# Keys transposed in fp32 two groups at once and split afterwards, the third column block copied out of PSUM, the second keys one group later

## The chip, the core and the metric

The kernel runs on one core of a Trainium2 chip. The metric is the device time of one execution in microseconds, as the median of several runs. The core has five engines that work side by side: TensorE (PE in the profile; its weight loads are PEld), VectorE (DVE), ScalarE (ACT), GpSimd (POOL) and SyncE (SP), which here only issues DMAs. Matrix products land in PSUM, eight banks of 128 partitions by 512 fp32 columns; everything else lives in SBUF.

## The reference

The model is an encoder of two layers over 1024 positions of width 1024: attention and an MLP, then a gated MLP and an MLP. The change lies in the first layer's attention, of which this is what matters:

```python
def gqa_attention(h, w_qkv, q_g, k_g, w_o, cos, sin):
    qkv = h @ w_qkv                                   # 1024 x (1024 + 256 + 256)
    q, k, v = jnp.split(qkv, [Q_WIDTH, Q_WIDTH + KV_WIDTH], axis=-1)
    q = apply_rope(rmsnorm(q.reshape(B, T, N_HEADS, HEAD_DIM), q_g), cos, sin)
    k = apply_rope(rmsnorm(k.reshape(B, T, N_KV_HEADS, HEAD_DIM), k_g), cos, sin)
    ...
    s = jnp.einsum('bqkgd,bskd->bkgqs', q_blk, k).astype(jnp.float32) * scale
    p = jax.nn.softmax(s, axis=-1).astype(v.dtype)
    return jnp.einsum('bkgqs,bskd->bqkgd', p, v)
```

There are 16 query heads and 4 key heads of 64 columns; each key head serves a group of four query heads.

## The kernel before

Products of fp32 precision are made of float32r products: each operand is split into a high part (the value cast to float32r) and a low part (the value minus the high part), and three products are summed: high by high, high by low, low by high. So each split costs a cast, on ScalarE, and a subtraction, mostly on VectorE.

The projection is cut in two halves of 512 positions (`hs` and `hs1` hold the split activations) and three column blocks of 512: block 0 is keys and values (256 + 256 columns), blocks 1 and 2 are the queries. `qkv_mm(cb, kp, ps, hp)` (L568) issues the 24 products of block `cb` for one pair `kp` of the eight depth slices, into four PSUM banks of 128 positions each; four calls make a block. `banks(False)` takes four banks of the pool that `bank_x` serves, `banks(True)` both buffers of the score pool `ps_s` (two of two banks each, also served one at a time by `bank_s`). So at most one block of each kind is under way, and the next block of that kind waits until everything that reads the banks of the last has been read.

The blocks run in this order, first half: 0 and 1 together, then 2, into `ps` of the score pool; second half: 0 (`pk`), 1 (`pq`, score pool), 2 (`ps`). What is done with a block:

- values (`values`, L605): split by ScalarE (L610) and VectorE (L611), straight out of PSUM.
- keys: copied out (`k_copies`, L588), roped by VectorE (`k_rows`, L657), scaled by GpSimd (`k_scale`, L660; the scale comes from squares on ScalarE, L622, and sums on VectorE, L623). The tile holds two blocks of 128 positions by 256 columns.
- then `k_split` (L665) writes each key head twice side by side, once as high parts (ScalarE, L671) and once as low parts (VectorE, L672): eight tiles of 128 x 512 for each half. `kstacks` (L676) transposes these: for each of four heads and for high and low, four float32r transposes of 128 x 128 (L681) into a bank, and a copy (L683) into a tile of `kst`. Each `kst` tile is then a head's keys, 64 rows, stacked twice over 512 positions.
- queries: block 1 is copied out of PSUM (`q_copies`, L597); block 2 of the first half (`ps` at L826 to L829) is not: its squares (L622) and its ropes (L633 and L635 on VectorE, with L636 adding on GpSimd) read PSUM. `qk_scale` (L649) scales on GpSimd.

The score stage (`s_stage`, L943) multiplies query tiles, which hold high and low parts stacked in 128 rows, by a head's two `kst` tiles of each half. The first queries get there through `q_stage` (L918), which splits them on GpSimd (L925, L926), and `q_trans` (L930), two groups of four transposes (L934) and a copy. `q_stage(0, 0)` and `q_trans` are called after `qkv_mm(2, 1, ps, hs1)`, and the first scores after `qkv_mm(2, 2, ...)`.

The order on each engine comes from a planner: it simulates the program and issues, among the instructions that are ready by its own costs, the one that comes first in the program. Slots of the tile pools (58 of tag `t`, 16 of tag `x`) are handed out as they come free. An instruction may be pinned behind the one traced before it on its engine: `hold` does so up to L822, and `pin` in the attention's stages (L934, L948, L965 and others). The projection's products of the second half, `kstacks`, the ropes and the splits are not pinned. The attention proper is an order written out by hand, over 64 units of one query head and 256 queries each.

Of the kernel before, what the change touches and what calls it, by code (L numbers as in the profile page):

```python
# [12 lines left out]
F32R = mybir.dt.float32r  # L13
AF = mybir.ActivationFunctionType
ALU = mybir.AluOpType
# [3 lines left out]
P = 128  # L19
# [5 lines left out]
NKV = 4  # L25
HD = 64
# [10 lines left out]
def encoder_kernel(ctx: ExitStack, tc: tile.TileContext, t: dict, out: bass.AP):  # L37
# [22 lines left out]
    def slot(dt=F32, shape=(P, 512)):  # L60
        return mem.tile(list(shape), dt, tag="t", name=nm("t"), bufs=SLOTS["t"])

    def xslot(dt=F32):
        return mem.tile([P, 512], dt, tag="x", name=nm("x"), bufs=SLOTS["x"])
# [21 lines left out]
    def f32(ap):  # L86
        return ap.bitcast(F32)
# [451 lines left out]
    kst = {}  # L539
# [3 lines left out]
    if True:  # L543
# [53 lines left out]
        def q_copies(ps):  # L597
            raws = []
            for j in range(4):
                raw = slot()  # L600
                S.copy(raw, ps[j])
                raws.append(raw)
            return raws
# [11 lines left out]
        def heads(ap, nt=1):  # L615
            return ap.rearrange("p (t h d) -> p t h d", t=nt, d=HD)
# [27 lines left out]
        def q_sums(src):  # L644
            return qk_rstd(qk_sums(src))
# [5 lines left out]
        def q_rope(hf, cb, src, r, js, add=None):  # L651
            for j in js:
                d = qk_rope(src[j], 0, hf * 4 + j, 1, V, add)
                qk_scale(d, r, j)
                qn[(hf * 4 + j, cb - 1)] = d

        def k_rows(hf, src):  # L657
            return [qk_rope(src[j], 1, hf * 4 + 2 * j, 2) for j in range(2)]
# [3 lines left out]
            for j in range(2):  # L662
                qk_scale(kd[j], r, j)

        def k_split(kd):  # L665
            kk = []
            for j in range(4):
                kh, kl = slot(F32R), slot(F32R)
                src = heads(kd[j // 2], 2)[:, j % 2].unsqueeze(2).broadcast_to([P, NKV, 2, HD])
                hv = kh.rearrange("p (g s d) -> p g s d", g=NKV, s=2)  # L670
                S.copy(hv, src)  # L671
                V.tensor_tensor(kl.rearrange("p (g s d) -> p g s d", g=NKV, s=2), src, f32(hv), ALU.subtract)  # L672
                kk.append((kh, kl))
            return kk

        def kstacks(hf, kk, bank):  # L676
            for g in range(NKV):
                for s in range(2):
                    pt = bank("kt", dt=F32R)
                    for j in range(4):  # L680
                        T.transpose(pt[:, j * P : (j + 1) * P], kk[j][s][:, g * P : (g + 1) * P], identr)  # L681
                    d_ = xslot(F32R)
                    S.copy(d_, f32(pt))  # L683
                    kst[(g, hf, s)] = d_

        row = wide("c")
        nc.sync.dma_start(row[0:1, :], t["cond"])
# [135 lines left out]

        pk = banks(False)
        qkv_mm(0, 0, pk, hs1)
        rr2 = q_sums(ps)  # L826
        q_rope(0, 2, ps, rr2, (0, 1), G)
        qkv_mm(0, 1, pk, hs1)
        q_rope(0, 2, ps, rr2, (2, 3), G)  # L829
        qkv_mm(0, 2, pk, hs1)  # L830
        qkv_w(2, 0, V, True)
        kk = k_split(kd)
        qkv_mm(0, 3, pk, hs1)
        rk = k_copies(pk)
        values(1, pk)
        pq = banks(True)
        qkv_mm(1, 0, pq, hs1)
        kd = k_rows(1, rk)
        qkv_w(2, 1, V, True)
        qkv_mm(1, 1, pq, hs1)  # L840
        kstacks(0, kk, bank_x)
        k_scale(kd, rk)
        kk = k_split(kd)
        qkv_mm(1, 2, pq, hs1)
        qkv_w(2, 2, V, True)
        q_rope(0, 1, r1, rr, (0, 1))
        qkv_mm(1, 3, pq, hs1)
        qkv_w(2, 3, V, True)
        r3 = q_copies(pq)
        kstacks(1, kk, bank_x)  # L850
        ps = banks(False)
        qkv_mm(2, 0, ps, hs1)
        q_rope(0, 1, r1, rr, (2, 3))
        rr = q_sums(r3)
        r1 = r3
# [60 lines left out]
    with ExitStack() as es:  # L916
# [127 lines left out]
        for j in range(4):  # L1044
            deferred[10 + j] = lambda j=j: late_rope1(j)
            deferred[2 + 2 * j] = lambda j=j: late_sums(j)
            deferred[3 + 2 * j] = lambda j=j: late_rope(j)
        del hs, hs1, xs, xs1, rb, rb1, ps, pk, pq, rk, kk, kd, sq0, sq1, wq, r3
        for i in range(nu + 2):
            u0 = units[i] if i < nu else None  # L1050
            u1 = units[i - 1] if 0 < i <= nu else None
# [799 lines left out]
```

## Time and profile before

| | |
|---|---|
| median of 3 runs | 2628.07 us (2626.15, 2628.07, 2628.24) |
| span of the profiled execution | 2625.8 us |
| the profiled execution's own time | not listed apart from the three runs; the span lies 0.35 us under the fastest of them |
| TensorE busy | 2601.6 us (99%) |
| VectorE, ScalarE, GpSimd busy | 2183.1, 1451.1, 723.2 us (83, 55, 28%) |
| mean granted TensorE clock | 0.999 |
| projection's second half and the start of the attention | about 90 to 170 us of the span |

How to read the lines shown below. A group's line has the source line, engine, operation, output and input names, shapes and count, then the busy time, the mean ns of one, and the idle time of the engine just before it with what ended it. A line of the timeline has its start in us, its length, engine, source line, operation and how many instructions are merged; a bracket gives the idle time before it and what ended that. Matmuls are pipelined and their shown lengths overlap, so the distance from start to start is what counts. A row of a stretch has its bounds and length, then the busy us of PE, PEld, DVE, ACT and POOL with the number of instructions, the granted clock (1.00 is full), the DMA share and GB/s. Where a line such as L575 is reached from many calls, the tile names tell which: `qkv<-s,t` and `qkv<-w,t` have their weights in the kept buffers (block 0, and block 2 in the second half), `qkv<-t,t` is block 1, and block 2 in the first half.

### The profile page before, as it was taken

Reading aid. Unit: us, or ns where it says so; the run is one execution under the profiler, and the core shown is the slowest. Engines: PE = TensorE matmul, PEld = TensorE weight load, DVE = VectorE, ACT = ScalarE, POOL = GpSimd, SP = SyncE. Lnnn points to the kernel's source line nnn. Section 1 sums busy time; section 2 is a strip of 40 time slices with the busy share of each in tenths; the row PEclk is TensorE's granted clock in tenths of the full one; section 3 lists DMA queues with packets and bytes.
Section 4 is the critical chain, followed back from the end, with each engine's and each line's share of the span. In section 5 each row is a group of like instructions: output and inputs, shape, how many; then the busy total and the mean of one; then the engine's idle time right before and its main releaser. Section 6 shows DMA issues by size and latency. Waiting matters only on the chain. (4 is left out here: it accounts for less than half of the span.)

```text
span 2625.8 us, 37307 instructions
## 1 busy us (share of the span) xinstructions
PE 2601.6 (99%) x12860; PEld 2172.2 (83%) x12860; DVE 2183.1 (83%) x3276; ACT 1451.1 (55%) x2612; POOL 723.2 (28%) x531
## 2 busy tenths in 40 slices
PE   9999999999999999999999999999999999999999
PEld 7789999888788888888888888888888788888887
DVE  7868999887989989877897687788979977789974
ACT  4569999854654455446543354445456645465442
POOL 0238776533000004430122054451520000005400
PEclk9999999999999999999999999999999999999999
DMA  8010222234486788545243355568641554487461
GB/s 306 27 33 9 74 88 75 97 112 145 168 288 245 270 310 306 192 133 172 82 136 121 120 174 175 178 204 305 237 141 50 177 179 156 153 310 268 149 211 58
DMA packets 208752, 435.39 MB, mean 166 GB/s; under 512 B 23025, under 2 KB 35441, under 8 KB 208562
## 3 DMA queue, kind: packets, MB, share of 16 engines
q1 hardware_dynamic: 181682, 395.24, 44.7%
q10 hardware_dynamic: 26880, 37.76, 4.0%
q8 instruction: 102, 1.67, 0.3%
q14 instruction: 88, 0.72, 0.1%
HBM read 310.23 MB, written 122.68 MB: 165 GB/s over the span
## 5 line engine op out<-in xcount | busy, mean ns | idle before, releaser
L1212 PE MATMUL out<-t,s 128*128 128x512 f32 x1232 | 479.9, 390 | 0.9 <-ACT t L328 0.8
L1213 PE MATMUL out<-t,s 128*128 128x512 f32 x1232 | 479.3, 389 | 0.7 <-DVE t L329 0.7
L1214 PE MATMUL out<-t,s 128*128 128x512 f32 x1232 | 478.9, 389 | 0.0
L469 PE MATMUL w<-t,s 128*128 128x512 f32 x1168 | 459.8, 395 | 0.9 <-ACT t L328 0.5
L470 PE MATMUL w<-t,s 128*128 128x512 f32 x1168 | 455.2, 390 | 1.8 <-DVE t L329 1.8
L471 PE MATMUL w<-t,s 128*128 128x512 f32 x1168 | 454.7, 389 | 0.0
L329 DVE TENSOR_TENSOR t<-t,t 128x512 fp32r<-128x512 f32 x408 | 324.7, 806 | 36.2 <-ACT t L328 29.0
L328 ACT CAST t<-t 128x512 fp32r<-128x512 f32 x408 | 245.3, 617 | 122.2 <-DMA t<-hf 71.7
L1213 PEld LDWEIGHTS out<-t,s 128*128 128x128 f32 x1232 | 231.2, 188 | 50.2 <-DVE t L329 1.8
L1212 PEld LDWEIGHTS out<-t,s 128*128 128x128 f32 x1232 | 231.2, 188 | 50.2 <-ACT t L328 1.7
L1214 PEld LDWEIGHTS out<-t,s 128*128 128x128 f32 x1232 | 231.2, 188 | 48.1
L454 ACT CAST s<-w 128x512 fp32r<-128x512 f32 x292 | 173.4, 616 | 161.4 <-PE w L471 104.3
L470 PEld LDWEIGHTS w<-t,s 128*128 128x128 f32 x1168 | 219.3, 188 | 49.7 <-DVE t L329 5.2
L469 PEld LDWEIGHTS w<-t,s 128*128 128x128 f32 x1168 | 219.3, 188 | 49.4 <-issue 2.9
L471 PEld LDWEIGHTS w<-t,s 128*128 128x128 f32 x1168 | 219.2, 188 | 45.6
L455 DVE TENSOR_TENSOR s<-w,s 128x512 fp32r<-128x512 f32 x292 | 221.8, 766 | 41.1 <-ACT s L454 40.6
L1194 ACT CAST s<-t 128x512 fp32r<-128x512 f32 x240 | 148.2, 620 | 187.0 <-PE out L1214 136.3
L1180 POOL TENSOR_TENSOR w<-w,t 128x512 f32<-128x512 f32 x20 | 34.2, 1721 | 767.7 <-DMA t<-hf 691.5
L1195 DVE TENSOR_TENSOR s<-t,s 128x512 fp32r<-128x512 f32 x240 | 195.1, 814 | 56.1 <-ACT s L1194 55.4
L951 DVE TENSOR_REDUCE mx<-s 128x1 f32<-128x1024 f32 x128 | 156.2, 1220 | 30.5 <-PE s L948 29.2
L974 DVE TENSOR_TENSOR t<-t,t 128x512 fp32r<-128x512 f32 x256 | 164.1, 681 | 17.1 <-ACT t L968 16.4
L984 PE MATMUL o<-t,t 128*128 128x256 f32 x1024 | 162.6, 291 | 0.0
(251 smaller groups left out, 5089.1 us busy)
## 6 DMA issues: line engine op xcount, KB each, us to landing
t<-hf SPq DMA_DIRECT2D x320, 256.0 KB, 4.0
hf<-c SPq DMA_DIRECT2D x156, 256.0 KB, 3.4
w<-in_wi_dram SPq DMA_DIRECT2D x64, 512.0 KB, 4.5
hf<-c ACTq DMA_DIRECT2D x96, 256.0 KB, 2.7
w<-in_ada_dram SPq DMA_DIRECT2D x36, 512.0 KB, 3.9
x<-in_ada_dram SPq DMA_DIRECT2D x64, 256.0 KB, 5.4
t<-in_wm_dram SPq DMA_DIRECT2D x64, 256.0 KB, 4.7
wf<-w SPq DMA_DIRECT2D x64, 256.0 KB, 3.0
```

What stands on the lines that cost most here:

```text
L328: S.copy(hi, src)
L329: (eng or V).tensor_tensor(lo, src, f32(hi), ALU.subtract)
L454: S.copy(hi, src)
L455: V.tensor_tensor(lo, src, f32(hi), ALU.subtract)
L469: T.matmul(ps, hi[:, a], th, start=kt == 0, stop=False)
L470: T.matmul(ps, hi[:, a], tl, start=False, stop=False)
L471: T.matmul(ps, lo[:, a], th, start=False, stop=kt == 3)
L974: pin(V.tensor_tensor(lo, pt, f32(hi), ALU.subtract))
L1195: V.tensor_tensor(lo, src, f32(hi), ALU.subtract)
L1212: T.matmul(ps, hi[:, a], th, start=begin and kt == 0, stop=False, **g)
L1213: T.matmul(ps, hi[:, a], tl, start=False, stop=False, **g)
L1214: T.matmul(ps, lo[:, a], th, start=False, stop=end and kt == 3, **g)
```

## The change

`k_split` is gone. `kstacks` now takes the fp32 key tiles themselves, and for each pair of key heads (128 columns) makes four fp32 transposes into one bank, with one head's keys in rows 0 to 63 and the other's in rows 64 to 127. From there each head's high part is cast by ScalarE twice, into the upper and the lower half of its `kst` tile, the low part is subtracted by VectorE out of PSUM into one half, and VectorE copies it into the other half. The block of query columns 2 of the first half is copied out of PSUM (`r2 = q_copies(ps)`), and its squares and ropes read the copy. The second half's `kstacks` moves from before to after `qkv_mm(2, 0, ...)` and takes its banks from the score pool.

```diff
--- before.py
+++ after.py
@@ -662,26 +662,20 @@
             for j in range(2):
                 qk_scale(kd[j], r, j)
 
-        def k_split(kd):
-            kk = []
-            for j in range(4):
-                kh, kl = slot(F32R), slot(F32R)
-                src = heads(kd[j // 2], 2)[:, j % 2].unsqueeze(2).broadcast_to([P, NKV, 2, HD])
-                hv = kh.rearrange("p (g s d) -> p g s d", g=NKV, s=2)
-                S.copy(hv, src)
-                V.tensor_tensor(kl.rearrange("p (g s d) -> p g s d", g=NKV, s=2), src, f32(hv), ALU.subtract)
-                kk.append((kh, kl))
-            return kk
-
-        def kstacks(hf, kk, bank):
-            for g in range(NKV):
-                for s in range(2):
-                    pt = bank("kt", dt=F32R)
-                    for j in range(4):
-                        T.transpose(pt[:, j * P : (j + 1) * P], kk[j][s][:, g * P : (g + 1) * P], identr)
-                    d_ = xslot(F32R)
-                    S.copy(d_, f32(pt))
-                    kst[(g, hf, s)] = d_
+        def kstacks(hf, kd, bank):
+            for gp in range(2):
+                pt = bank("kt")
+                for j in range(4):
+                    src = kd[j // 2][:, (j % 2) * 256 + gp * P : (j % 2) * 256 + (gp + 1) * P]
+                    T.transpose(pt[:, j * P : (j + 1) * P], src, ident)
+                for i in range(2):
+                    a, b = 64 * i, 64 - 64 * i
+                    hi, lo = xslot(F32R), xslot(F32R)
+                    S.copy(hi[a : a + 64], pt[a : a + 64])
+                    S.copy(hi[b : b + 64], pt[a : a + 64])
+                    V.tensor_tensor(lo[a : a + 64], pt[a : a + 64], f32(hi[a : a + 64]), ALU.subtract)
+                    V.tensor_copy(lo[b : b + 64], f32(lo[a : a + 64]))
+                    kst[(2 * gp + i, hf, 0)], kst[(2 * gp + i, hf, 1)] = hi, lo
 
         row = wide("c")
         nc.sync.dma_start(row[0:1, :], t["cond"])
@@ -823,33 +817,32 @@
 
         pk = banks(False)
         qkv_mm(0, 0, pk, hs1)
-        rr2 = q_sums(ps)
-        q_rope(0, 2, ps, rr2, (0, 1), G)
+        r2 = q_copies(ps)
+        rr2 = q_sums(r2)
+        q_rope(0, 2, r2, rr2, (0, 1), G)
         qkv_mm(0, 1, pk, hs1)
-        q_rope(0, 2, ps, rr2, (2, 3), G)
+        q_rope(0, 2, r2, rr2, (2, 3), G)
         qkv_mm(0, 2, pk, hs1)
         qkv_w(2, 0, V, True)
-        kk = k_split(kd)
         qkv_mm(0, 3, pk, hs1)
         rk = k_copies(pk)
         values(1, pk)
         pq = banks(True)
         qkv_mm(1, 0, pq, hs1)
-        kd = k_rows(1, rk)
+        kd0, kd = kd, k_rows(1, rk)
         qkv_w(2, 1, V, True)
         qkv_mm(1, 1, pq, hs1)
-        kstacks(0, kk, bank_x)
+        kstacks(0, kd0, bank_x)
         k_scale(kd, rk)
-        kk = k_split(kd)
         qkv_mm(1, 2, pq, hs1)
         qkv_w(2, 2, V, True)
         q_rope(0, 1, r1, rr, (0, 1))
         qkv_mm(1, 3, pq, hs1)
         qkv_w(2, 3, V, True)
         r3 = q_copies(pq)
-        kstacks(1, kk, bank_x)
         ps = banks(False)
         qkv_mm(2, 0, ps, hs1)
+        kstacks(1, kd, bank_s)
         q_rope(0, 1, r1, rr, (2, 3))
         rr = q_sums(r3)
         r1 = r3
@@ -1045,7 +1038,7 @@
             deferred[10 + j] = lambda j=j: late_rope1(j)
             deferred[2 + 2 * j] = lambda j=j: late_sums(j)
             deferred[3 + 2 * j] = lambda j=j: late_rope(j)
-        del hs, hs1, xs, xs1, rb, rb1, ps, pk, pq, rk, kk, kd, sq0, sq1, wq, r3
+        del hs, hs1, xs, xs1, rb, rb1, ps, pk, pq, rk, kd, kd0, sq0, sq1, wq, r3
         for i in range(nu + 2):
             u0 = units[i] if i < nu else None
             u1 = units[i - 1] if 0 < i <= nu else None
```

## The prediction

> **What bounds the kernel now.** I read the page first.
>
> ```profile
> span 2625.8 us, 37307 instructions
> PE 2601.6 (99%) x12860; PEld 2172.2 (83%) x12860; DVE 2183.1 (83%) x3276; ACT 1451.1 (55%) x2612; POOL 723.2 (28%) x531
> ```
>
> TensorE is busy nearly everywhere, so time goes away only where TensorE's own work shrinks or where it stood still. A change in one stage is worth what TensorE loses in that stage. The changed lines run between about 98 and 170 us, so next I asked for busy time and granted clock by stretches there (columns: PE, PEld, DVE, ACT, POOL, clock, DMA).
>
> ```profile
> 111.30:113.60 2.30, 0.19 (x2) 0.04 (x1) 2.30 (x6) 2.09 (x4) 1.62 (x2) 1.00 0.00 0
> 113.60:126.30 12.70, 12.70 (x48) 10.03 (x48) 12.70 (x17) 3.12 (x10) 9.13 (x7) 0.87 0.00 0
> 115.00:118.50 3.50, 3.50 (x10) 2.69 (x10) 3.50 (x5) 0.11 (x1) 3.34 (x4) 0.51 0.00 0
> ```
>
> There is one hole in TensorE's row, and a stretch at half the granted clock soon after it. VectorE is full through both (2.30 of 2.30, 12.70 of 12.70); ScalarE is not. TensorE's timeline shows what the hole waits for, and the two groups of key transposes.
>
> ```profile
> 111.09 0.39 PE L577 MATMUL qkv<-w,t 128*128 128x512 f32 x1
> 113.59 0.47 PE L575 MATMUL qkv<-t,t 128*128 128x512 f32 x1 [2.11 <-DVE t L635]
> 115.05 0.60 PE L575 MATMUL qkv<-t,t 128*128 128x512 f32 x1
> 126.31 3.23 PE L681 MATMUL kt<-identr,t 128*128 128x128 f32 x32
> 129.38 0.47 PE L575 MATMUL qkv<-t,t 128*128 128x512 f32 x1
> 140.37 1.49 PE L681 MATMUL kt<-identr,t 128*128 128x128 f32 x16
> 142.19 2.01 PE L681 MATMUL kt<-identr,t 128*128 128x128 f32 x16 [0.33 <-ACT x L683]
> 144.15 0.50 PE L575 MATMUL qkv<-s,t 128*128 128x512 f32 x1
> ```
>
> At 113.59 the projection's next block wants the PSUM banks that the third column block of the first half still holds; VectorE's rope (L633, L635) reads them there.
>
> **Transposes on TensorE.** Before: 64 float32r transposes, 126.31 to 129.38 and 140.37 to 144.15, which is 3.07 + 3.78 = 6.85 us, the 0.33 us wait included. After: 16 fp32 ones. The trace has that form in the attention:
>
> ```profile
> 169.51 1.03 PE L965 MATMUL t<-ident,c 128*128 128x128 f32 x8
> 170.30 1.17 PE L948 MATMUL s<-x,t 128*128 128x512 f32 x4
> ```
>
> Eight take 0.79 us, as much apiece as the float32r form (3.07/32 = 0.096 us), so 16 take 1.6 us. Saved: 5.3 us. More than 6.85 can't come from here.
>
> **The hole.** With the third block copied out, the banks are free once ScalarE has made four copies. The ones it makes of the other blocks cost, beside the casts that the change touches:
>
> ```profile
> L601 ACT COPY t<-qkv 128x512 f32<-128x512 f32 x8 | 4.3, 592 | 3.8 <-PE qkv L577 3.8
> L671 ACT CAST t<-t 128x512 fp32r<-128x512 f32 x8 | 4.5, 616 | 6.8 <-POOL t L636 4.7 <-POOL t L649 2.1
> L683 ACT CAST x<-kt 128x512 fp32r<-128x512 f32 x16 | 8.0, 636 | 1.8 <-PE kt L681 1.8
> L994 ACT COPY t<-o x64: 364/368/374, 179.8 to 555.6; 64x256 f32<-64x256 f32 x64
> L593 ACT COPY t<-qkv 128x256 f32<-128x256 f32 x4 | 1.2, 387 | 0.6 <-PE qkv L576 0.6
> 103.75 2.04 ACT L622 ACTIVATE t<-qkv 128x512 f32<-128x512 f32 x4
> ```
>
> Four copies are 2.4 us. ScalarE reads this block at 103.75 in the row of squares, so even done there the copies end near 106.2, five us ahead of the need at 111.3. The hole of 2.11 us goes; what is late next is the chain of the queries, below. ScalarE elsewhere loses eight casts of 616 ns and sixteen of 636 (15.1 us) and gains sixteen half-height copies. The rows of L994 and L593 show that half the partitions save nearly nothing (368 against 387 ns), so at about 0.6 us each these are 9.6 us. With the four copies its work falls by about 3 us; under cover of TensorE either way.
>
> **The half clock.** The 48 matmuls of 113.59 to 126.31 take 12.72 us; the next 48, from 129.38 to 140.37, take 10.99. The difference, 1.7 us, is the stretch at 0.51. It begins 3.6 us after TensorE went idle. The other hole of this size in the trace is followed by the same, and the long gapless stretches show none:
>
> ```profile
> 500.55 1.59 PE L965 MATMUL t<-ident,c 128*128 128x128 f32 x7 [1.89 <-ACT c L957]
> 502.00:504.00 2.00, 2.00 (x7) 1.51 (x7) 0.75 (x2) 2.00 (x4) 2.00 (x4) 0.50 0.69 168
> 2044.28 0.50 PE L469 MATMUL w<-t,t 128*128 128x512 f32 x1 [1.19 <-ACT t L328]
> ```
>
> (1.19 us at 2044 leaves the clock alone.) So a hole of about 1.9 us or more halves the clock for some 3.4 us, and without the hole I count the 1.7 us as saved. [...]
>
> Gross, on TensorE: 5.3 + 2.1 + 1.7 = 9.1 us.
>
> **What it lays on VectorE and the queries' chain.** This is where I expect some of it back. The score stage needs the first queries turned, and these come from VectorE's rope of the first column block (138.58 to 148.83), GpSimd's scaling, and GpSimd's split:
>
> ```profile
> 135.99 2.67 DVE L672 TENSOR_TENSOR t<-t,t 128x512 fp32r<-128x512 f32 x4 [1.88 <-ACT t L671]
> 138.58 0.68 DVE L633 TENSOR_TENSOR t<-t,t 128x512 f32<-128x512 f32 x1
> 148.14 0.69 DVE L636 TENSOR_TENSOR t<-t,t 128x512 f32<-128x512 f32 x1
> 143.41 1.36 POOL L649 TENSOR_TENSOR t<-t,r 128x512 f32<-128x512 f32 x1 [0.69 <-DVE t L636]
> 149.99 0.74 POOL L925 CAST t<-t 128x256 fp32r<-128x256 f32 x2
> 152.77 1.44 POOL L926 TENSOR_TENSOR t<-t,t 128x256 fp32r<-128x256 f32 x2
> 155.16 0.80 PE L934 MATMUL qt<-identr,t 128*128 128x128 f32 x8
> ```
>
> GpSimd ends at 154.21 and TensorE wants the result at 155.16: 0.95 us to spare. With 9.1 us gone TensorE is there at 146.1. How far does the chain move? VectorE loses eight subtractions and one wait:
>
> ```profile
> L672 DVE TENSOR_TENSOR t<-t,t 128x512 fp32r<-128x512 f32 x8 | 7.7, 996 | 1.9 <-ACT t L671 1.9
> L974 DVE TENSOR_TENSOR t<-t,t 128x512 fp32r<-128x512 f32 x5 | 3.2, 683 | 0.0
> L93 DVE CAST identr<-ident 128x128 fp32r<-128x128 f32 x1 | 0.2, 220 | 0.0
> 118.83 1.53 DVE L672 TENSOR_TENSOR t<-t,t 128x512 fp32r<-128x512 f32 x1
> 118.43 1.38 POOL L649 TENSOR_TENSOR t<-t,r 128x512 f32<-128x512 f32 x1
> 111.20 0.68 DVE L633 TENSOR_TENSOR t<-qkv,t 128x512 f32<-128x512 f32 x1
> 111.36 1.27 POOL L636 TENSOR_TENSOR t<-t,t 128x512 f32<-128x512 f32 x1 [4.92 <-DVE e L248]
> 146.51 1.60 DVE L635 TENSOR_TENSOR t<-t,t 128x256 f32<-128x256 f32 x2
> ```
>
> That is 7.7 + 1.9 = 9.6 us. Each half of the keys brings four subtractions out of PSUM and four copies within SBUF. A subtraction out of PSUM is L974's row, 0.68 us. The trace has no SBUF copy of 512 columns; the nearest is L93's 0.22 us for 128 columns. Four times that, 0.88, bounds it from above and 0.22 from below; I take 0.55. So one half costs 3.6 to 6.2, taken as 4.9 us. The first half's falls ahead of the queries' ropes. The second half's is issued between the two pairs of ropes, at a time when its transposes have hardly run, so I take it to come behind the last rope (0), and up to 6.2 if it goes first.
>
> The copied third block has a price too. A subtraction with both inputs in SBUF takes 1.53 us beside a GpSimd instruction (118.83) and 0.67 alone (2.67/4). The rope that reads PSUM takes 0.68 us beside one (111.20). After the change that rope has both inputs in SBUF. [...] Three of the four ropes meet GpSimd. One rope could lose 0.85 on its 512-wide product and 0.92 on its two 256-wide ones (1.60 at 146.51 against 0.68 for as many columns in one), so 1.8 each, 5.3 in all. Before the change the same GpSimd work already slowed other instructions, which now run later and alone, so the lower end is 0. I take 2.
>
> The chain moves by -9.6 + 4.9 + 2 = -2.7 us; its ends are -9.6 + 3.6 = -6.0 and -9.6 + 6.2 + 6.2 + 5.3 = +8.1. GpSimd would then end at 151.5, and TensorE at 146.1 waits up to 5.4 us. Two things shorten that. The split of the first queries needs only the first two ropes; issued behind their scalings, which end at 144.77, its 4.2 us would end at 149.0 before and 146.3 after. And the 24 matmuls that follow the query transposes (half of the 10.99 us above, 5.5) depend on nothing here; they are not pinned, so the planner may put them first. Between 0.2 and 5.4 us I take 2.5 lost.
>
> **Second keys one group later.** They take no time of their own: their transposes move behind 24 matmuls, into banks that the copies of the first column block free, and the scores that read them come another 48 matmuls later. The scaled keys were ready at 136.3 (134.26 and 2.05 us on):
>
> ```profile
> 134.26 2.05 POOL L649 TENSOR_TENSOR t<-t,r 128x512 f32<-128x512 f32 x2 [11.29 <-DVE r L250]
> ```
>
> TensorE finishes the first column block 6.1 us earlier (hole, half clock and the first key group: 2.1 + 1.7 + 3.07 - 0.8), at 134.3 instead of 140.4, and 5.5 later, at 139.8, it reaches the keys: cover of 3.5 us, and a later key chain would cost what it exceeds that by. The change adds no DMA and moves no queue but VectorE's.
>
> **Sum.** -9.1 + 2.5 = -6.6 us: the span goes from 2625.8 to about 2619.2. The execution of the trace lies 2.3 us under the median of the three runs, 2628.07, and 0.35 under their fastest; the difference carries over, so 2621.5 for the median.
>
> **Rivals.** First, the queries set the time. If the planner keeps the order and the whole 5.4 us are waited out, that hole is long enough to halve the clock once more (1.7): -9.1 + 7.1 = -2.0, 2626.1. For it: VectorE full, 0.95 us to spare. Against: two ways to fill. Chance 0.27.
>
> Second, slower: the upper end of the chain. [...] GpSimd then ends 8.1 us later than before, at 162.3, which is 7.1 past the 155.16 of now, and the clock halves again: +7.1 + 1.7 = 8.8, 2636.9. It decides from the point where the chain is 4.5 us later than now (5.3 less 1.7, and the 0.95 to spare). Against it: the 9.6 us that go are sure, and the additions would all have to lie at their ends. Chance 0.10.
>
> Third, the half clock is not the hole's doing and stays: 6.6 - 1.7 = 4.9 saved, 2623.2. For it: only two holes to judge by. [...] Chance 0.08.
>
> Fourth, the copy doesn't do what it says: ScalarE makes it too late for the block at 111.3, as it waits for buffers at L671 (4.7 us in its row). Then hole and half clock stay, TensorE reaches the queries at 149.9 and waits 1.6 for 151.5: 5.3 - 1.6 = 3.7 saved, 2624.4. Chance 0.05.
>
> **How the numbers follow.** The forecast has 0.50. About 0.2%, 5.3 us, is what a measurement of this kernel can tell from no change. The forecast is beyond it; a few of the third and first cases, with the wait partly filled, are too (0.07): faster 0.57. The rest of the first, third and fourth is within it: 0.33. The second is slower: 0.10. All of the gross sum kept gives 2619.0, and the runs spread by 2 us, so the range begins at 2617.5; it ends at 2630, past the first rival and the milder part of the second, and leaves out about 0.15.
>
> **What would show it.** Right: no idle before L575 at the first column block of the second half and clock 1.00 behind it; sixteen key transposes with about 0.1 us each; ropes of the third block reading a t tile and longer than 0.68 us. The step I trust least is the wait before the query transposes: over 4 us there, or a second half-clock stretch near 150 us, and the first or second rival is true.

## The result, and the profile after

| | before | after |
|---|---|---|
| median, 19 runs each on the same chips | 2627.03 us (2623.98 to 2629.14) | 2631.10 us (2627.86 to 2634.42) |
| ratio, 95% interval | | 1.0016 (1.0010 to 1.0022) |
| span of the profiled execution | 2625.8 us | 2627.7 us |

The change costs 4.1 us, or 0.16%; 2621.5 us was forecast, with a range of 2617.5 to 2630. The page of the kernel after:

```profile
span 2627.7 us, 37214 instructions
PE 2596.6 (99%) x12812; PEld 2168.5 (83%) x12812; DVE 2192.5 (83%) x3284; ACT 1449.9 (55%) x2608; POOL 723.8 (28%) x531
```

TensorE's work fell by 5 us (2601.6 to 2596.6) and by 48 matmuls, as the new stacks should make it, and still the span grew: TensorE stands still longer. The busy times by stretch of the kernel after (PE, PEld, DVE, ACT, POOL, granted clock, DMA) show where:

```profile
111.30:113.60 2.30, 2.30 (x12) 1.91 (x11) 2.30 (x5) 1.71 (x5) 1.70 (x1) 1.00 0.00 0
113.60:124.00 10.40, 8.85 (x40) 7.05 (x39) 10.40 (x11) 2.45 (x7) 9.21 (x7) 1.00 0.00 0
148.20:151.63 3.43, 0.00 (x0) 0.00 (x0) 3.37 (x6) 0.23 (x1) 2.88 (x5) 1.00 0.00 0
151.63:155.04 3.41, 0.22 (x2) 0.25 (x2) 3.14 (x8) 2.32 (x4) 1.75 (x3) 0.50 0.00 0
155.04:158.45 3.41, 2.01 (x10) 1.31 (x10) 2.31 (x5) 1.75 (x3) 0.00 (x0) 0.50 0.00 0
158.45:161.87 3.42, 3.42 (x10) 2.74 (x10) 0.00 (x0) 1.87 (x2) 0.00 (x0) 0.50 0.00 0
161.87:165.30 3.43, 3.43 (x16) 2.79 (x16) 0.00 (x0) 0.00 (x0) 0.00 (x0) 1.00 0.43 141
```

The hole at 111.5 us is gone (2.30 of 2.30 busy) and the clock behind it is full (1.00). A new hole fills 148 to 155 us, and from 151.63, inside it, to 161.87 the granted clock is 0.50. TensorE's timeline of the kernel after names what is waited for (in brackets the idle time and what ended it):

```profile
123.90 1.06 PE L670 MATMUL kt<-ident,t 128*128 128x128 f32 x8 [1.55 <-DVE t L611]
124.72 0.48 PE L575 MATMUL qkv<-t,t 128*128 128x512 f32 x1
141.16 1.04 PE L670 MATMUL kt<-ident,t 128*128 128x128 f32 x8
141.96 0.48 PE L575 MATMUL qkv<-s,t 128*128 128x512 f32 x1
154.82 0.72 PE L927 MATMUL qt<-identr,t 128*128 128x128 f32 x4 [7.17 <-DVE x L676]
157.93 0.72 PE L927 MATMUL qt<-identr,t 128*128 128x128 f32 x4 [1.40 <-DVE x L676]
165.16 1.07 PE L941 MATMUL s<-x,t 128*128 128x512 f32 x4
```

L670 is the new key transpose, L927 the query transpose (L934 before), L941 the scores. The bracket of 7.17 us does not name the queries' split on GpSimd. It names L676, the subtraction that takes the low part of a *key* out of PSUM. VectorE's, ScalarE's and GpSimd's timelines of the kernel after, each a fence, show how late that is:

```profile
145.88 1.59 DVE L635 TENSOR_TENSOR t<-t,t 128x256 f32<-128x256 f32 x2
148.59 1.86 DVE L623 TENSOR_REDUCE qss<-t 128x8 f32<-128x512 f32 x3
151.22 0.68 DVE L676 TENSOR_TENSOR x<-kt,x 64x512 fp32r<-64x512 f32 x1
153.98 0.69 DVE L676 TENSOR_TENSOR x<-kt,x 64x512 fp32r<-64x512 f32 x1
157.09 0.69 DVE L676 TENSOR_TENSOR x<-kt,x 64x512 fp32r<-64x512 f32 x1 [0.79 <-ACT x L675]
```

```profile
142.39 0.58 ACT L675 CAST x<-kt 64x512 fp32r<-64x512 f32 x1
151.22 0.23 ACT L245 ACTIVATE y<-qss 128x32 f32<-128x32 f32 x1 [8.24 <-DVE qss L641]
151.93 0.58 ACT L674 CAST x<-kt 64x512 fp32r<-64x512 f32 x1 [0.48 <-DVE x L676]
```

```profile
149.75 1.40 POOL L919 TENSOR_TENSOR t<-t,t 128x256 fp32r<-128x256 f32 x2
151.79 1.58 POOL L919 TENSOR_TENSOR t<-t,t 128x256 fp32r<-128x256 f32 x2
```

The second keys are transposed at 141.16 and the first pair of casts ends at 142.97, so VectorE could subtract from then on. Its order has the last ropes (L635) and four sums of squares (L623) first, and the subtraction starts at 151.22. The keys stand in the two score buffers until then, and the query transposes want those same two buffers. Once the two subtractions of the first buffer are done (153.98 + 0.69 = 154.67), TensorE goes on, at 154.82.

The first queries were not what was missing. `q_stage(0, 0)` makes two casts and two subtractions; GpSimd ends the subtractions at 151.15 (149.75 + 1.40). The row at 151.79 is already the next head group, which the attention asks for later. (Expectations below that have the queries' split end at 153 to 154 us mean that row.) TensorE was free at 147.65, so the queries alone would have held it for 3.5 us; the buffers held it for 7.2.

ScalarE adds to the hold in two ways. The casts of a bank's second head start only when the first head has been subtracted (151.93 behind 151.22 + 0.68); this holds for all four banks of keys, with 8.5 us of ScalarE's idle time in all. The runs show it, not why; where the split is made from SBUF ("keys copied", below), ScalarE makes the eight casts without a stop, from 144.79 to 149.90. And in the second half all casts but the first pair stand behind the inverse root (L245 at 151.22), which waits for VectorE's sums. With that order on ScalarE an earlier first subtraction alone would not have freed a buffer.

### The profile page after: what moved, and what is told of

It reads as the page before. It is cut to its first block, busy times and chain, and to the rows that moved or that the text cites. A ratio compares the mean times of both kernels' runs of the same rounds, so it can differ in the third digit from the quotient of the medians.

```text
span 2627.7 us, 37214 instructions
## 1 busy us (share of the span) xinstructions
PE 2596.6 (99%) x12812; PEld 2168.5 (83%) x12812; DVE 2192.5 (83%) x3284; ACT 1449.9 (55%) x2608; POOL 723.8 (28%) x531
## 4 chain that ended last, share of the span: by engine, by line
PE 85%; DVE 9%; ACT 2%; DMA 2%; issue 1%; POOL 0%; SPq 0%; DVEq 0%; ACTq 0%
PE out L1205 10%; PE out L1207 10%; PE out L1206 10%; PE w L469 10%; PE w L470 10%; PE w L471 10%; PE s L941 4%; PE o L977 4%; PE t L958 3%; PE v L1562 3%; PE v L1564 3%; PE v L1563 3%; PE mix L1654 2%; DVE t L329 1%; ACT c L950 1%
```

## The experiments

**How they are read.** The first projection matmul starts anywhere from 17.8 to 21.4 us in the eighteen profiled executions, before any changed line. So each profile is read by the time from that matmul (L575) to the first transposes of probabilities, the first step behind all that the change touches. The four rows for it, kernel before, then kernel after (the row at 169.51 stands in the prediction):

```profile
19.45 0.50 PE L575 MATMUL qkv<-s,t 128*128 128x512 f32 x1 [0.77 <-ACT t L303]
```

```profile
19.25 0.50 PE L575 MATMUL qkv<-s,t 128*128 128x512 f32 x1 [0.77 <-ACT t L303]
173.32 1.03 PE L958 MATMUL t<-ident,c 128*128 128x128 f32 x8
```

That is 150.06 us before and 154.07 after: +4.0, where the medians differ by 4.1. All runs, the stretch read in the same way:

| kernel | stretch against before, us | median, us (kernel before on the same chip) | ratio, 95% interval |
|---|---|---|---|
| after | +4.0, again +4.1 | 2631.10 (2627.03) | 1.0016 (1.0010 to 1.0022) |
| split early | +4.1 | 2631.94 (2626.74) | 1.0021 (1.0012 to 1.0030) |
| two buffers | +3.8 | 2631.37 (2626.74) | 1.0019 (1.0010 to 1.0028) |
| both of these | +5.0 | 2632.00 (2626.74) | 1.0020 (1.0012 to 1.0029) |
| keys back | +1.6 | 2629.28 (2626.74) | 1.0013 (1.0004 to 1.0022) |
| copy alone | +4.7 | 2632.41 (2626.95) | 1.0021 (1.0012 to 1.0030) |
| stacks alone | -1.7, again -1.4 | 2628.90 (2626.49) | 1.0008 (0.9999 to 1.0016) |
| keys copied | -0.9 | 2627.26 (2626.95) | 1.0005 (0.9997 to 1.0014) |
| keys copied, split early | -0.7 | 2627.42 (2626.95) | 1.0002 (0.9993 to 1.0011) |
| order alone | -3.2 | 2625.92 (2626.49) | 0.9996 (0.9987 to 1.0005) |
| order, split early | -5.4 | 2623.22 (2626.95) | 0.9987 (0.9978 to 0.9996) |
| order, split early, sums late | -6.8 | 2622.34 (2626.49) | 0.9985 (0.9976 to 0.9994) |
| keys copied, split early, sums late | -8.1, again -7.3 | 2622.50 (2626.49) | 0.9984 (0.9975 to 0.9993) |
| the same without the third block's copy | -5.6 | 2623.93 (2625.64) | 0.9992 (0.9983 to 1.0001) |

My theory after the result: the late subtractions hold the buffers. The rival was the one that the prediction had feared: the queries' chain (rope, scale, split) sets the time.

**Split early.** `q_stage(0, 0)` is called right behind the first two ropes; its definition moves up.

```diff
         q_rope(0, 1, r1, rr, (0, 1))
+        qh = q_stage(0, 0)
...
-        qh = q_stage(0, 0)
         nxt = []
```

> The changed kernel, but the split of the first queries on GpSimd is called right after the first two ropes of the first column block instead of after the projection's second-last group; banks as in the changed kernel. If the queries' chain alone is the cause, the split ends near 148, the hole goes, about 2622. If the banks alone, or both one behind the other, the query transposes still start near 154.7 and the median stays within 1 us of 2631.

GpSimd has the first queries split at 144.86, and TensorE waits as before. GpSimd's and TensorE's timelines of this kernel:

```profile
144.07 0.79 POOL L688 TENSOR_TENSOR t<-t,t 128x256 fp32r<-128x256 f32 x1
```

```profile
154.22 0.72 PE L928 MATMUL qt<-identr,t 128*128 128x128 f32 x4 [7.65 <-DVE x L676]
```

The queries are ready 9.4 us before TensorE gets to turn them, and its wait is 7.65 us, not shorter. In the changed kernel the chain is not what is late.

**Two buffers.** Both key groups go into one score buffer of two banks, both query groups into the other.

```diff
+    def two_banks(dt=F32):
+        b = ps_s.tile([P, SEQ], dt, tag="s", name=nm("two"))
+        halves = [b[:, :512], b[:, 512:]]
+        return lambda s, dt=F32: halves.pop(0)
...
-        kstacks(1, kd, bank_s)
+        kstacks(1, kd, two_banks())
...
+        bank_q = two_banks(F32R)
-        q_trans(qh, 0, nxt, bank_s)
+        q_trans(qh, 0, nxt, bank_q)
```

> The changed kernel, but the second keys' two groups of transposes share one buffer of the score pool (its two banks), and the two groups of query transposes share the other. No instruction is added or left out. In the changed kernel the query transposes stood idle 7.17 and 1.40 us, both ended by VectorE's subtraction out of the keys' banks, and half the clock followed. If the banks alone are the cause, the first query transposes start near 148 instead of 154.8, without a hole, and the median falls by some 9 us, to about 2622. If the queries' own chain (GpSimd's split, which ended at 153.37) stands right behind the banks, they start near 153.5, the second group follows at once, and only the 1.3 and 1.4 us go with little of the half clock: about 2628 to 2629.

And with the split early as well:

> Both edits: separate buffers and the early split. If banks and chain together are the cause, the hole before the query transposes shrinks below 1 us, no half clock follows, and the gross sum of the prediction comes out: 2627.0 less 7 to 9, so 2618 to 2620. If something else holds the query transposes (the second group's banks, a wait of TensorE for weights), the hole stays above 4 us and the time above 2625.

With the buffers alone neither time that was expected came; with both edits it is the second case, that something else holds the query transposes. The hole only moved: now the second group of keys waits for the subtractions of the first, 9.07 us alone and 9.54 us with the split early. A buffer shared by both groups ties the second to the first. These two don't tell the theories apart; they show again that VectorE's subtractions come late.

**Keys back.** Only "one group later" is undone.

```diff
         r3 = q_copies(pq)
+        kstacks(1, kd, bank_x)
         ps = banks(False)
         qkv_mm(2, 0, ps, hs1)
-        kstacks(1, kd, bank_s)
```

> The changed kernel with only its third part undone: the second keys are transposed ahead of the next column block again, in the other pool's banks. If the move one group later (into the score pool's banks) is what costs, the query transposes no longer wait for VectorE's subtraction, but for GpSimd's split near 153.5; the key transposes wait some 2.5 us for the scaled keys (ready near 138.3) and the block behind them for the banks that VectorE still reads. I expect 2627 to 2629: better than the changed kernel by 2 to 4, no better than before. If the move helps, it is slower than 2631.

No query transpose waits, but TensorE, early by the savings, now meets other late things:

```profile
PE kt L670 <- POOL t L649: 3.7, 2, 3.2
PE qkv L575 <- DVE x L676: 1.6, 2, 1.1
PE kt L670 <- DVE t L611: 1.6, 1, 1.6
```

(Waits of this kernel: total us, times, longest.) The keys aren't scaled yet, and the next block's banks hold keys not yet subtracted. Moving the keys answered a real want, and cost more than it answered: +4.0 against +1.6 in the stretch. (The intervals of the two medians overlap.)

**The parts alone.** The copy of the third block in the kernel before, and the new stacks at the old places (their diff is the `kstacks` of the change with `bank_x` for both).

```diff
-        rr2 = q_sums(ps)
-        q_rope(0, 2, ps, rr2, (0, 1), G)
+        r2 = q_copies(ps)
+        rr2 = q_sums(r2)
+        q_rope(0, 2, r2, rr2, (0, 1), G)
```

> The kernel before with one part of the change alone: ScalarE copies the third column block of the projection's first half out of PSUM; keys are transposed as before and at the old place. Theory 1 (the late subtractions hold the score buffers only where the second keys stand in them): no hole of 7 us can come, since the second keys keep the old bank; the 2.1 us hole at 111.5 and the 1.7 us of half clock behind it go, and what the queries' chain takes is only the part beyond 0.95 us of cover: first scores between 157.6 and 160.5 (161.35 before), time 0.8 to 3.8 us below before. Theory 2 (the queries' chain sets the time whatever is saved earlier): the 3.8 us stand again as idle time ahead of the first query transposes, first scores at 161.4, time within 1 us of before.

The stacks alone:

> The kernel before with one part of the change alone: the new key stacks (four transposes in place of sixteen for two groups), both at their old places and in the old banks; the third column block stays in PSUM, so the hole at 111.5 us stays with its half clock. Theory 1 (VectorE, over 95% busy from 100 to 147 us, is what TensorE waits for here, so each TensorE saving turns into a wait): the eight subtractions and eight copies (about 9 us of VectorE where the four subtractions from SBUF went) come out as new holes ahead of key transposes or of the blocks behind them, first scores at 160.5 to 163, time within 2 us of before. Rival, the prediction's sum: 5.3 us of TensorE go, less what the queries' chain takes beyond 0.95 us: first scores at about 156 to 160.4, time 1 to 5 us below before.

The copy removes the hole at 111.5 and brings a threefold one, in this row of its TensorE timeline:

```profile
130.49 4.30 PE L681 MATMUL kt<-identr,t 128*128 128x128 f32 x32 [6.54 <-DVE t L611]
```

The key transposes want the banks of the keys' and values' block, and VectorE reads the values there (L611) only at 130.03 us, behind ropes that had got longer. Both theories had missed this. The stacks alone keep the hole at 111.5 and get one of 3.65 us for L676 at 144.31 (2.04 in a second execution); the stretch falls by 1.4 to 1.7 us, of the 5.3 that TensorE saved. The rest went into the wait for VectorE and the half clock behind it (0.91 granted from 140 to 147 us, 0.87 from 147 to 155). Neither expectation holds whole: the scores at 158.84 fit the rival, the median fits neither.

**Keys copied, and split early.** ScalarE copies the second keys' banks to SBUF, so no subtraction holds a bank; then the split is early as well.

```diff
             pt = bank("kt")
...
+                if hf:
+                    raw = slot()
+                    S.copy(raw, pt)
+                    pt = raw
```

> The changed kernel, but ScalarE copies the second keys' two banks to SBUF and the split into high and low parts is done from there, so a bank is free after its first two copies and waits for no subtraction of VectorE. Theory 1 (the banks alone held the query transposes): the 7.17 and 1.40 us of idle time go to under 1 us, first scores at about 156 to 158, time 4 to 6 us below before. Theory 2 (the queries' chain stands right behind the banks): the query transposes still wait, now for GpSimd's split that ends at about 153 to 154, some 5 to 6 us of idle time stay, first scores at about 162 to 163 and the time is 0.5 to 2 us above before.

With the split early:

> The kernel of the run with the second keys copied by ScalarE, and the first queries' split issued right behind the first two ropes as well, so both suspected holds are gone. Theory 1 and 2 alike, if these are the only two holds: idle time ahead of the query transposes under 1 us, no second stretch at half clock, first scores at 154.5 to 156.5 (161.35 before, 165.16 with the change), time 4.5 to 7 us below before, that is 2620 to 2622.5. Rival (a third wait stands behind both, or what is saved before 165 us is given back by the half clock or the hole near 500 us): first scores as early as said, but the time less than 3 us below before.

With the banks free the queries' chain stands behind them (4.62 us for GpSimd's L923 in the first kernel, its scores at 162.07, as the second theory had it). Its TensorE and GpSimd timelines:

```profile
157.38 1.09 PE L931 MATMUL qt<-identr,t 128*128 128x128 f32 x7 [4.62 <-POOL t L923]
```

```profile
156.59 0.73 POOL L923 TENSOR_TENSOR t<-t,t 128x256 fp32r<-128x256 f32 x1
157.97 1.42 POOL L923 TENSOR_TENSOR t<-t,t 128x256 fp32r<-128x256 f32 x2
```

The transposes follow the second subtraction (156.59 + 0.73 = 157.32) and do not wait for the pair at 157.97, which is the next head group's. That second subtraction was late because GpSimd's order has the scaling of the last rope (L649, 155.59) in front of it, and this waited for VectorE. With the split early too, a third thing stands behind both, in the second kernel's TensorE and ScalarE timelines:

```profile
157.31 2.07 PE L946 MATMUL s<-x,t 128*128 128x512 f32 x4 [3.95 <-ACT t L935]
```

```profile
156.56 0.23 ACT L245 ACTIVATE y<-qss 128x32 f32<-128x32 f32 x1 [6.85 <-DVE qss L641]
156.69 1.05 ACT L935 CAST t<-qt 128x512 fp32r<-128x512 f32 x2
```

The query transposes run at 147.05, but ScalarE's copies of them (L935) are queued behind an inverse root (L245) that waits 6.85 us for VectorE's sums. The 2620 to 2622.5 that I had expected was wrong: there were three holds in a row, not two.

**VectorE's order.** No operation is added; `pinned` keeps the last ropes and sums behind the keys' subtractions.

```diff
         kstacks(1, kd, bank_s)
+        pinned[0] = True
         q_rope(0, 1, r1, rr, (2, 3))
         rr = q_sums(r3)
+        pinned[0] = False
```

> The changed kernel with VectorE's order alone changed (second keys ahead of ropes three and four), the first queries' split left at its old place, behind all four ropes. Theory 1 (two holds, one behind the other: the banks, then the queries' chain): the subtractions come early and the banks are free at about 147 to 150, but GpSimd's split now waits for the later ropes and ends at about 158 to 160, so the query transposes wait some 7 to 10 us for it, with a half clock behind; time 2 to 6 us above before. Rival (the banks were all): query transposes without a wait over 1 us, time 2 to 5 us below before.

With the split early:

> The changed kernel with the first queries' split issued right behind the first two ropes, and the other two ropes and the sums behind them put later in VectorE's order than the second keys' four subtractions and copies: no operation added, only VectorE's order changed. Theory 1 (banks held by the late subtractions): subtractions at about 142 to 145 instead of 151 to 157, query transposes at 147 to 148, first scores at 155 to 157.5, time 4 to 6.5 us below before. Rival (the order only moves the wait: ropes and sums that come later hold the second queries or the exponentials): a new hole of 2 us or more between 148 and 175 us, and a time within 2 us of before.

These with "after" and "split early" make a table of two by two: medians 2631.1 (neither), 2631.9 (split early), 2625.9 (order), 2623.2 (both). The order is worth 5 to 9 us, the split nothing without it. With the order alone GpSimd's split ends at 158.0 (156.59 + 1.42), and TensorE waits 2.69 us, not the 7 to 10 that I had written: the planner had filled the rest with projection products. The time is that of before within the interval, not 2 to 6 us above. The first subtraction and the query transposes of this kernel:

```profile
143.68 0.68 DVE L676 TENSOR_TENSOR x<-kt,x 64x512 fp32r<-64x512 f32 x1 [0.39 <-ACT x L675]
```

```profile
157.37 0.28 PE L929 MATMUL qt<-identr,t 128*128 128x128 f32 x1 [2.69 <-POOL t L921]
```

With both, the scores start at 159.99, later than expected, since the projection began 1.9 us later in this execution (21.36) and ScalarE's copies of the queries are late here too (0.93 us of wait). The edit also puts ScalarE's inverse root behind the casts of the keys (157.45 with the order alone); no run tells what VectorE's order is worth without that.

**Sums late.** `q_sums` of the last block moves behind the query transposes.

```diff
-        rr = q_sums(r3)
...
         q_trans(qh, 1, nxt, bank_s)
+        rr = q_sums(r1)
```

> The kernel with the second keys copied by ScalarE and the first queries' split early, with one step moved: the sums of squares of the last projected column block come behind the query transposes in program order, so ScalarE's two copies of the transposed queries stand ahead of the inverse root that waits for VectorE's sums. Theory 1 (in the run without this move the 3.95 us of idle time ahead of the first scores and the half clock behind it were that order and nothing else): no idle time over 1 us there, clock 1.00, first scores at 153 to 155, time 4.5 to 7 us below before. Rival (VectorE is the bound, so the time comes back elsewhere): a new hole of 2 us or more before 175 us, time within 3 us of before.

The same move where VectorE's order was changed:

> The kernel whose VectorE does the second keys ahead of the last two ropes, with the same one step moved: the last sums of squares behind the query transposes. Theory 1: the 0.93 us ahead of the first scores goes and nothing else changes before 175 us; first scores at 155 to 159, time 4 to 6 us below before (3.7 below without this move). Rival (the first softmax then starts no earlier, since VectorE is busy with ropes until about 157 us): the same time as without the move within 1 us.

In the first of the two kernels ScalarE copies the queries at 146.80 and the scores start at 152.46 without a wait (161.35 before):

```profile
146.30 0.80 PE L931 MATMUL qt<-identr,t 128*128 128x128 f32 x8
152.46 1.07 PE L945 MATMUL s<-x,t 128*128 128x512 f32 x4
```

So the third hold was that order. In the second the scores start at 153.38, earlier still than the range given, and the median is 4.2 us below before. That is within 1 us of the kernel without the move (3.7 below), as that run's rival had it, though the stretch is 1.4 us shorter. Both kernels beat the two given ones, by about 4 us against before and about 8 against after.

**Size still open, and the copy once the holds are gone.** Three kernels in a second profiled execution, first the changed one:

> The changed kernel, unaltered, in a second profiled execution. Theory 1 (the waits of the first 550 us are the program's own; the stretch behind the first output projection differs from execution to execution): the same 7.2 and 1.4 us ahead of the query transposes, first scores at 164.5 to 165.5; from the first to the last matmul behind 546 us any time between 2074.6 and 2080.5 us, the bounds seen so far. Rival (that stretch belongs to the kernel too): 2074 to 2075 us again, and first scores as said.

The stacks alone:

> The kernel with the new key stacks alone, unaltered, in a second profiled execution. Theory 1 (the late stretch differs from execution to execution): the same holes of 2.1 and 3.7 us before 145 us, first scores at 158.5 to 159.2; the late stretch, 2080.5 us before, shorter by 2 us or more. Rival (the late stretch is the kernel's): 2080 to 2081 us again, and with it the explanation of a time that stays above before although its scores come 2.5 us earlier.

Keys copied, split early, sums late:

> The fastest kernel so far (second keys copied by ScalarE, split early, last sums late), unaltered, in a second profiled execution. Theory 1: first scores at 152.2 to 152.8; the late stretch, 2074.6 us before, longer by 2 us or more, which would explain a median 4.5 us above its first profiled execution. Rival: 2074 to 2075 us again.

And that kernel with `q_sums` and `q_rope` of the third block on `ps` again, as before the change:

> The kernel with second keys copied by ScalarE, split early and sums late, but without one part of the change: VectorE reads the third column block from PSUM, as before the change. Theory 1 (with the later holds gone, what TensorE saves earlier counts): the hole of about 2.1 us at 111.5 is back, with 1.7 us of half clock behind it, less the 1.55 us wait for the values at about 123 that came only because TensorE was early: first scores at 153.5 to 156.5, time 1 to 4 us above the kernel with the copy, that is 0 to 3 us below before. Rival (VectorE bounds the stretch, so TensorE's 3.8 us are worth nothing): first scores at 152 to 153.5 and the time as with the copy, within 1 us.

The stretch repeats to within 0.8 us in all three kernels; the changed kernel's wait is 7.19 us again. The three executions took 2630.23, 2628.57 and 2619.76 us. The absolute times of the scores that I had written missed in all three (166.71, 161.46 and 153.51), in two because the start of the projection had moved (20.74 and 20.95 us). From the first output projection matmul to the last matmul the stacks alone took 2080.9 us and then 2076.0, the changed kernel 2075.1 and 2073.2 (below the bounds I gave), the fastest kernel 2075.0 and 2076.0 (not the 2 us more that I expected). So this part differs by up to 5 us between executions of the same program, which hides differences of the size in question; by itself it doesn't explain why the fastest kernel's median gains 4.0 us (interval 1.8 to 6.6) where its stretch gains 7.3 to 8.1. That, and the time of the stacks alone, stay open.

Without the third block's copy the stretch is 1.7 to 2.5 us longer: the copy that cost 4.7 us alone is worth about 2 once nothing late stands behind it (scores at 154.92, in the first theory's range). Of this 1.7 is the stretch at half clock that followed the hole in the profiled execution (0.50 for the 3.41 us from 113.64 to 117.05); the medians (4.0 and 1.7 us below before) have intervals that overlap.

## Why the prediction was wrong

- **Transposes: right.** Eight fp32 transposes take 0.82 and 0.80 us (123.90 to 124.72, 141.16 to 141.96), 1.6 for both groups.
- **The hole: right,** but 1.55 us came back as a wait for the values (L611), at the first key transposes, which the prediction did not have.
- **Gross sum: nearly right.** TensorE was free for the query transposes at 147.65 (154.82 - 7.17) instead of 155.16: 7.5 us, and 9.1 less 1.55 is 7.55.
- **The step that failed** is "Second keys one group later. They take no time of their own: their transposes move [...] into banks that the copies of the first column block free". It asked when those banks come free and not who wants them next. Those are the query transposes, and they wait until VectorE has subtracted the second keys. That VectorE would do so behind the last rope, the prediction had chosen itself, as the harmless case (0 for the queries' chain). It was the harmful one: 7.17 + 1.40 us of idle time. From 147.65 to the first scores at 165.16 there are 17.5 us; from 155.16 to 161.35 there were 6.2. Of the 11.3 more, 8.6 are these waits, and the remaining 2.7 are put down to the half clock (0.50 from 151.63 to 161.87, in which TensorE was busy for 5.64 us: half of that is 2.8). 11.3 - 7.5 is the 3.8 by which the scores come later.
- **The queries' chain: misread and of another size, and it wasn't what bound.** The prediction took 154.21 for the end of the first queries' split. That is the end of the next head group's; before the change the first queries were ready at 152.13 (150.69 + 1.44, the row below), 3.0 us ahead of TensorE and not 0.95. Its own sum then gives a wait of up to 3.4 us instead of 5.4. The split ended at 151.15 after, 1.0 us earlier, where -2.7 was forecast. The term that failed is the ropes from SBUF, taken as +2. The third and fourth rope of the third block took VectorE 2.5 us from PSUM (113.36 to 115.88) and 7.3 from SBUF (113.77 to 121.06): 4.8 more for two ropes, where the bound was 1.8 for each. With 4.8 in place of 2 the prediction's sum for VectorE is +0.1 instead of -2.7, and the last rope did end within 0.2 us of before (148.66 against 148.83). The rows, GpSimd's before, then VectorE's before and after:

```profile
150.69 1.44 POOL L926 TENSOR_TENSOR t<-t,t 128x256 fp32r<-128x256 f32 x2
```

```profile
113.36 0.67 DVE L633 TENSOR_TENSOR t<-qkv,t 128x512 f32<-128x512 f32 x1
115.88 1.33 DVE L672 TENSOR_TENSOR t<-t,t 128x512 fp32r<-128x512 f32 x1
```

```profile
113.77 1.53 DVE L633 TENSOR_TENSOR t<-t,t 128x512 f32<-128x512 f32 x1
115.22 2.70 DVE L635 TENSOR_TENSOR t<-t,t 128x256 f32<-128x256 f32 x2
121.06 0.68 DVE L566 TENSOR_TENSOR s<-c,s 128x512 fp32r<-128x512 f32 x1
```

- The key half, taken as 4.9 us, is 4.9 (5.5 + 4.3 for eight subtractions and eight copies).
- **The two things that were to shorten the wait** did not: the planner left the 24 products behind the query transposes, and the split's last part stayed behind the late scaling.
- **The first and second rival** had the place (a wait before the query transposes, a second half-clock stretch near 150 us) but not the cause: both had the queries late. So the sign of being wrong that the prediction gave came, and pointed at the wrong cause. In the changed kernel the queries would have cost 3.5 us at most; the first rival comes true only when the buffers are freed, as the keys-copied run shows. The fourth did not come, since the hole at 111.5 is gone.

## What to carry to other kernels

When a step is moved into other buffers, list everything that uses those buffers next and the last reader on the slowest engine, and price that wait as carefully as the move. Where an engine beside TensorE has no idle time in a stage (VectorE here, 10.40 of 10.40 us), TensorE's savings can become waits until that engine's order is mended; here a change of VectorE's order was worth 5 to 9 us, and of the 5 us of TensorE work removed, the stacks alone kept 1.4 to 1.7 in the stretch and nothing that the median shows. Price a bank that two engines read in turn as the sum of both: with the order alone the first bank of the second keys was read from 142.47 to 146.29 us, for four casts of 0.58 and two subtractions of 0.68. After one hold is freed, ask for the next: here there were three, on three engines.

## What the runs showed of the hardware

- **A stretch at half clock followed some of TensorE's holes and not others.** In the kernel before the granted clock was 0.50 for 3.41 us from 115.06 and for 3.42 from 500.76, in the changed kernel for 10.24 us (151.63 to 161.87). The hole at the third block's banks was 2.11 to 2.13 us long in four executions. In three a stretch at 0.50 came behind it: before, the stacks alone the second time, and the kernel without the third block's copy. In the first execution of the stacks alone the clock stayed at 1.00. The stacks alone, first execution, then second:

```profile
108.24:111.65 3.41, 2.16 (x10) 1.46 (x8) 3.41 (x12) 1.55 (x6) 1.27 (x1) 1.00 0.00 0
111.65:115.06 3.41, 2.55 (x11) 2.15 (x12) 3.41 (x10) 1.70 (x6) 2.81 (x3) 1.00 0.00 0
115.06:118.47 3.41, 3.41 (x16) 2.83 (x16) 3.41 (x5) 0.14 (x1) 3.33 (x3) 1.00 0.00 0
```

```profile
112.80:116.22 3.42, 1.29 (x7) 0.89 (x6) 3.42 (x9) 2.54 (x8) 2.64 (x3) 1.00 0.00 0
116.22:119.63 3.41, 3.41 (x10) 2.63 (x9) 3.41 (x6) 0.37 (x1) 3.33 (x3) 0.50 0.00 0
```

  In the first, TensorE is idle for 1.25 and 0.86 us of the first two rows, 2.11 together, and all three rows have the full clock; in the second it is idle for 2.13 us of one row, and the next is at half. So the length of a hole alone doesn't decide it, and no run shows what does. The prediction's "about 1.9 us or more" holds for its two holes (2.11 and 1.89 us) and fails for the 2.11 us of the first execution above. Of shorter waits, the 1.55 us at 123.90 in the changed kernel left the clock at 1.00 (113.60 to 151.60), as did the 1.19 at 2044 before. The wait of 1.40 us at 157.93 in the changed kernel lies within its 10.24 us at half clock; what it adds to them is not shown. A lower clock also came with little idle time: from 400 to 500 us it was 0.98 in three of the seven kernels read there (keys back, copy alone, keys copied with the split early; TensorE idle for 0.48, 0.50 and 1.11 us of the 100), and 1.00 in the kernel before, idle for 1.82. That stays unexplained. So the 1.7 us that the prediction counted as saved were lost behind three of four such holes; its third rival, that the hole had no part in it, doesn't hold: with the hole gone the clock is 1.00 there (113.60 to 124.00 in the changed kernel).
- Half the partitions saved nothing on ScalarE or VectorE here: the 64x512 cast out of PSUM took 0.58 us in the changed kernel (0.59 for a 128x512 copy before), the 64x512 subtraction 0.69 (0.68 for 128x512 before).
